# Layer 1's modulation scale on VectorE, for both condition vectors, in two column halves

## The chip, the cores and the metric

The kernel runs on one core of a Trainium2 chip. Each core has a matrix engine (TensorE, PE in the profile; PEld is its weight load), a vector engine (VectorE, DVE), an activation engine (ScalarE, ACT), a general engine (GpSimd, POOL) and a queue engine (SyncE, SP) that here issues the loads. Each engine works through its own instructions in a fixed order and waits where a semaphore tells it to. The metric is the device time of one execution, in microseconds (us), as the median of several runs. TensorE's full clock was granted for nearly all of the execution (0.984 of it on average).

## The reference

A stack of four layers on a sequence x and a context ctx, 256 tokens of 2048 channels each. Ahead of every layer, the two condition vectors c (for x) and c_ctx (for ctx) are turned into a shift, a scale and a gate of 2048 numbers each: one product of a vector with a 2048 x 6144 weight per layer.

```python
def ada_modulation(cond, w, b):
    m = jax.nn.silu(cond) @ w + b
    return jnp.split(m, 3, axis=-1)          # shift, scale, gate

for i in range(DEPTH):
    shift, scale, gate = ada_modulation(c, ada_w[i], ada_b[i])
    h = rms_norm(x, norm_g[i]) * (1.0 + scale[:, None, :]) + shift[:, None, :]
    shift_c, scale_c, gate_c = ada_modulation(c_ctx, ada_w[i], ada_b[i])
    hc = rms_norm(ctx, norm_g[i]) * (1.0 + scale_c) + shift_c
    # o, oc = mixer of h, hc: Fourier (layers 0, 3), window attention (1), gated convolution (2)
    x = x + gate[:, None, :] * o
    if i < DEPTH - 1:
        ctx = ctx + gate_c * oc
return rms_norm(x, final_g)
```

The modulation of layers 0 and 1 is needed for both condition vectors; in layer 1 the shift and the scale for both, the gate for c alone, because after layer 1 nothing reads the context any more. Layers 2 and 3 need c alone. Every weight is float32, and 429.56 MB are read from memory in one execution.

## The kernel before

Every large product (each layer's input products and its output product) streams its weight in pieces of [128, 2, 512] through SP's queue (`w_piece`, line 147). Each piece is split into a rounded part `whi` (ScalarE, line 183) and a rest `wlo` (VectorE, or GpSimd in some stages, line 184), and three matmuls (lines 196 to 198, or 216 to 218) multiply them with activations that are split the same way. A product takes 8 pieces for each of its 512-column chunks, and TensorE can start on a piece only when both parts of it are there.

The modulation runs in between. It is cut into **thirds** (l, s): layer l, and s = 0 for the shift, 1 for the scale, 2 for the gate. A third is 16 **row pieces**, each 128 rows of `ada_w` by 2048 columns, loaded as two tiles `aw` of 128 x 1024 (512 KB each, four buffers, line 331). Layer 0's shift and scale are made by `ada_tiles` (line 223). All other thirds belong to one of two streams:

- `ada_a` (line 373) works on TensorE: (0, 2), (1, 0), (1, 1). A row piece is four fp32 matmuls of 512 columns with the two condition vectors as the stationary operand (line 273), next to each other in the columns of the array, so both vectors are done at once. They show as eight records per row piece in the trace.
- `ada_v` (line 374) works on VectorE, for c alone: (1, 2), then all thirds of layers 2 and 3. A row piece is two operations over 128 x 1024: accumulator `adacc` plus `aw` times one number per partition (line 286; the first row piece only multiplies, line 284). During layer 2's gated product the stream is switched to TensorE (`ada_v.pe`, line 1084).

At the end of a third `ada_group` sums `adacc` over the partitions with four fp32 matmuls against a column of ones (line 300), where VectorE took part; copies the rows out of PSUM on ScalarE (line 303); turns them into columns with four small matmuls (line 305); and adds the bias (line 311) and, for a scale, the 1 and the norm's weight (line 315). `adacc` has one buffer: a third's first VectorE operation waits until the third ahead has been summed.

How far a stream is to be at which place is set by hand. A product calls a pump between its pieces, and `plan(quarters, steps)` spreads row pieces over those steps until so many quarters of a third (four row pieces each) are done. The constants (lines 27 to 36) are these goals, counted over the whole list of the stream: `TZ`, `T0U`, `T0O` for `ada_v` in layer 0's gate product z, its product u and its output product; `T1` up to layer 1's z product; `T1O` for its output product; `T2`, `T2Z`, `T2O` for layer 2's gated product, z product and output product. `A0Z` and `A0U` are the same for `ada_a`. `until(l, s)` emits whatever of a third is still missing, at the place where it is needed. In program order `until(1, 1)` stands ahead of the build of layer 1's input (line 808), `until(1, 2)` ahead of layer 1's output product (line 1040), `until(3, 1)` behind layer 2's output product (line 1173).

Program order is a priority, not the final order: a scheduler places every engine's instructions at compile time, and fills what it takes for free time of an engine with later work whose buffers are free. Weight splits and the builds at a layer's start get a higher priority (lines 178 and 466). So row pieces run well ahead of their place in the program, as far as the four `aw` tiles and the one `adacc` allow.

## Time and profile before

| | |
|---|---|
| median of 3 runs | 1947.56 us (1942.82 to 1949.57) |
| span of the profiled execution (first to last instruction) | 1946.4 us |
| TensorE matmuls, busy | 1866.9 us (96%) |
| VectorE, busy | 1425.8 us (73%) |
| ScalarE, busy | 891.3 us (46%) |
| GpSimd, busy | 280.8 us (14%) |
| loads by SP's queue | 429.99 MB, 67.2% of 16 DMA engines' time |
| modulation tiles `aw` loaded by the two streams | 320 of 512 KB |
| VectorE operations on `adacc` | 202 (188 of line 286, 14 of line 284) |
| records of line 273, of line 300, of line 305 | 472, 56, 80 |

The profile shows one execution. Busy time is the time in which an engine works on an instruction; matmuls are pipelined and overlap, so TensorE's busy time is no measure of its throughput. The chain of waits is found by going back from the last instruction, at each step to what released it. A row of a group of instructions has the line, the engine, the operation, what is written and read with its shape, the count, then the busy time, the mean time of one in ns, and the idle time of the engine just before them with its cause.

The stages, from where the accumulators of the products are first and last written: layer 0's z until 278 us, its u until 510, its output product until 726; layer 1's attention until about 963, its z until 1090, its output product until 1195; layer 2's gated product until 1397, its z with the layer norm until about 1510, its output product until 1615; layer 3 after that.

### The profile page before, as it was taken

To read this page: it belongs to the slowest core of one execution; us is meant where nothing else is said; L and a number is where in the kernel's file an instruction comes from. 1 tells how busy PE (TensorE), PEld (TensorE's weight loads), DVE (VectorE), ACT (ScalarE), POOL (GpSimd) and SP (SyncE) were. 2 spreads that over 40 slices of the span, in tenths; PEclk is the share of its full clock that TensorE was granted. 3 is DMA by queue.
4 is the path that set the end of the run, shared out by engine and by line. 5 is a ranking of instruction groups with operands and counts; after the bars stand their busy time and mean duration, and the time that the engine had idled before them with its cause. 6 is when DMAs were issued, how large, how long until landed. Compare 5 with 4: busy or idle time off the path is not lost.

```text
span 1946.4 us, 31356 instructions
## 1 busy us (share of the span) xinstructions
PE 1866.9 (96%) x11911; PEld 1552.1 (80%) x11911; DVE 1425.8 (73%) x2639; ACT 891.3 (46%) x1591; POOL 280.8 (14%) x143
## 2 busy tenths in 40 slices
PE   6999999999999999999999998999997997999997
PEld 5566657777766787766789997999997997888897
DVE  3799944556654459977897766688899968897665
ACT  6433342224322235465565444444445546556553
POOL 0000000000000000000000003889887001000000
PEclk9999999999999999999999999999998998999999
DMA  8888877676677845822567775577776785886564
GB/s 246 273 303 296 301 247 269 208 234 212 228 268 267 279 127 163 306 88 84 178 219 246 253 245 164 186 228 230 230 225 196 273 279 168 286 270 176 160 173 131
DMA packets 221129, 433.72 MB, mean 223 GB/s; under 512 B 14678, under 2 KB 85046, under 8 KB 220978
## 3 DMA queue, kind: packets, MB, share of 16 engines
q1 hardware_dynamic: 219552, 429.99, 67.2%
q8 instruction: 93, 1.52, 0.3%
q10 hardware_dynamic: 1426, 1.73, 0.3%
q14 instruction: 58, 0.48, 0.1%
HBM read 429.56 MB, written 2.10 MB: 222 GB/s over the span
## 4 chain that ended last, share of the span: by engine, by line
PE 81%; DVE 7%; DMA 6%; ACT 2%; issue 2%; SPq 1%; POOL 1%; DVEq 0%; ACTq 0%; POOLq 0%
PE acco L196 7%; PE acco L198 7%; PE acco L197 7%; PE accz L196 7%; PE accz L197 7%; PE accz L198 6%; PE accu L216 4%; PE accu L217 4%; PE accu L218 4%; DMA aw<-in_ada_w_dram 3%; PE pa L273 3%; PE accg L196 3%; PE accg L197 3%; PE accg L198 3%; PE po L968 2%
## 5 line engine op out<-in xcount | busy, mean ns | idle before, releaser
L183 ACT CAST whi<-raw 128x512 fp32r<-128x512 f32 (+1 forms) x748 | 538.4, 769 | 719.1 <-PE acco L197 200.4
L184 DVE TENSOR_TENSOR wlo<-raw,whi 128x512 fp32r<-128x512 f32 x648 | 472.5, 777 | 238.1 <-ACT whi L183 235.2
L184 POOL TENSOR_TENSOR wlo<-raw,whi 128x1024 fp32r<-128x1024 f32 x100 | 256.0, 2568 | 1348.7 <-ACT whi L183 1336.1
L196 PE MATMUL acco<-yh,whi 128*128 128x256 f32 (+1 forms) x1040 | 323.1, 311 | 0.0
L198 PE MATMUL acco<-yh,wlo 128*128 128x256 f32 (+1 forms) x1040 | 320.7, 309 | 0.8 <-DVE wlo L184 0.8
L286 DVE SCALAR_TENSOR_TENSOR adacc<-aw,csil,adacc 128x1024 f32<-128x1024 f32 x188 | 255.0, 1362 | 85.9 <-DMA aw<-in_ada_w_dram 85.5
L198 PE MATMUL accz<-hx,wlo 128*128 128x256 f32 x768 | 221.7, 289 | 14.1 <-POOL wlo L184 13.4
L197 PE MATMUL accz<-hx,whi 128*128 128x256 f32 x768 | 221.7, 289 | 3.8 <-DVE hx L448 3.8
L196 PE MATMUL accz<-hx,whi 128*128 128x256 f32 x768 | 221.3, 289 | 1.1 <-ACT hx L447 1.1
L196 PEld LDWEIGHTS acco<-yh,whi 128*128 128x128 f32 x1040 | 197.6, 190 | 27.1 <-ACT whi L183 11.2
L197 PE MATMUL acco<-yh,whi 128*128 128x256 f32 x768 | 217.5, 283 | 0.0
L1113 DVE SCALAR_TENSOR_TENSOR pv<-gp,dwT,pv 128x256 f32<-128x256 f32 x480 | 190.9, 484 | 24.9 <-ACT pv L1107 24.5
L198 PEld LDWEIGHTS acco<-yh,wlo 128*128 128x128 f32 x1040 | 197.5, 190 | 11.6 <-DVE wlo L184 1.9
L198 PEld LDWEIGHTS accz<-hx,wlo 128*128 128x128 f32 x768 | 150.9, 197 | 16.0 <-POOL wlo L184 13.8
L197 PEld LDWEIGHTS accz<-hx,whi 128*128 128x128 f32 x768 | 151.0, 197 | 5.7 <-DVE hx L448 4.4
L196 PEld LDWEIGHTS accz<-hx,whi 128*128 128x128 f32 x768 | 150.9, 197 | 3.8 <-ACT hx L447 1.8
L198 PE MATMUL accg<-hx,wlo 128*128 128x256 f32 x512 | 145.8, 285 | 1.9 <-POOL wlo L184 1.9
L196 PE MATMUL accg<-hx,whi 128*128 128x256 f32 x512 | 146.7, 287 | 0.6 <-ACT whi L183 0.4
L197 PEld LDWEIGHTS acco<-yh,whi 128*128 128x128 f32 x768 | 146.5, 191 | 0.0
L197 PE MATMUL accg<-hx,whi 128*128 128x256 f32 x512 | 145.8, 285 | 0.6 <-DVE hx L448 0.5
L196 PEld LDWEIGHTS accg<-hx,whi 128*128 128x128 f32 x512 | 98.9, 193 | 8.7 <-issue 6.9
L197 PE MATMUL acco<-yl,whi 128*128 128x512 f32 (+1 forms) x272 | 102.8, 378 | 0.0
(257 smaller groups left out, 3474.5 us busy)
## 6 DMA issues: line engine op xcount, KB each, us to landing
aw<-in_ada_w_dram SPq DMA_DIRECT2D x376, 512.0 KB, 5.3
raw<-in_four_w_in_dram SPq DMA_DIRECT2D x126, 512.0 KB, 4.6
raw<-in_attn_w_in_dram SPq DMA_DIRECT2D x72, 512.0 KB, 4.1
raw<-in_four_w_out_dram SPq DMA_DIRECT2D x64, 512.0 KB, 4.9
raw<-in_conv_w_in_dram SPq DMA_DIRECT2D x128, 256.0 KB, 3.0
raw<-in_attn_w_out_dram SPq DMA_DIRECT2D x32, 512.0 KB, 4.1
raw<-in_conv_w_in_dram SPq DMA_DIRECT2D x32, 512.0 KB, 4.1
raw<-in_conv_w_out_dram SPq DMA_DIRECT2D x32, 512.0 KB, 4.9
```

Of the source, the lines that this page charges most:

```text
L183: nc.scalar.copy(hv[:, c], iv[:, c])
L184: eng.tensor_sub(lv[:, c], iv[:, c], hv[:, c].bitcast(F32))
L196: mm(o, a, hh, start=st, stop=False, skip_group_check=True)
L197: mm(o, a, hl, start=False, stop=False, skip_group_check=True)
L198: mm(o, b, hh, start=False, stop=kt + k == span[1] - 1, skip_group_check=True)
L216: mm(acc[:], hh, whi[:, k, :], start=st, stop=False)
L217: mm(acc[:], hh, wlo[:, k, :], start=False, stop=False)
L218: mm(acc[:], hl, whi[:, k, :], start=False, stop=kt + k == KT - 1)
L273: mm(pa[32 * g:32 * g + cs.shape[-1], :], cs, aw[g // 2][:, 512 * (g % 2):512 * (g % 2) + 512], start=fp, stop=kt == KT - 1, skip_group_ch ...
L286: ins = nc.vector.scalar_tensor_tensor(acc[:, cs], aw[i][:], cc, acc[:, cs], op0=ALU.mult, op1=ALU.add)
L968: mm(po[64 * h:64 * h + 64, :256], vt[k][:, g * 64:(g + 1) * 64], pTs[h][:, k, :, :].rearrange("p m q -> p (m q)"), start=k == 0, stop=k == 3,
L1113: nc.vector.scalar_tensor_tensor(pv[:, :256], gt[:, t:t + 256], dwT[:, kt, t:t + 1], pv[:, :256], op0=ALU.mult, op1=ALU.add)
```

## The change

Third (1, 1) leaves `ada_a` and becomes the first of `ada_v`, under the name `BOTH`. It gets a function of its own, because VectorE has to make it for both condition vectors, which TensorE did at once: the 2048 numbers of the accumulator are now 1024 columns for c and the same 1024 columns for c_ctx, and the third is made in two column halves, one behind the other. A half is 16 tiles `aw` of 128 x 1024, and each tile feeds two VectorE operations, one per vector. Two tiles count as one row piece in the plans, so the third still has 16. Each half is summed, copied, turned and finished by itself. The goals of both streams change with it; since `ada_v`'s list is four quarters longer at its head, a goal of 24 now stands for what 20 was.

```diff
-A0U = 7.5
-T0U = 6.5
-T0O = 9
-T1 = 14.25
-T1O = 17.5
-T2 = 20.25
-T2Z = 21
-T2O = 21
+BOTH = (1, 1)
+A0U = 5.5
+T0U = 6
+T0O = 9.5
+T1 = 15
+T1O = 20
+T2 = 23.25
+T2Z = 24
+T2O = 24
...
-TZ = 3
+TZ = 2
...
+    def ada_both(l, s, st):
+
+        w = D // 2
+        for h in range(2):
+            acc = cp.tile([P, D], F32, tag="adacc", name=nm("adacc"))
+            for k2 in range(0, KT, 2):
+                for kt in (k2, k2 + 1):
+                    aw = st.half(l, s, kt, h)
+                    for o in range(2):
+                        cs, cc = slice(w * o, w * o + w), csil[:, kt, o:o + 1]
+                        if kt == 0:
+                            ins = nc.vector.tensor_scalar(acc[:, cs], aw[:], cc, None, op0=ALU.mult)
+                        else:
+                            ins = nc.vector.scalar_tensor_tensor(acc[:, cs], aw[:], cc, acc[:, cs],
+                                                                 op0=ALU.mult, op1=ALU.add)
+                if k2 < KT - 2:
+                    yield
+            pa = rs_bank("pa")
+            for g in range(4):
+                mm(pa[32 * g:32 * g + 32, :], one0[:], acc[:, 512 * g:512 * g + 512],
+                   start=True, stop=True, skip_group_check=True)
+            a = tmp()
+            nc.scalar.copy(a[:], pa[:])
+            for j in range(4):
+                mm(pa[:, 8 * j:8 * j + 8], a[:, j * P:(j + 1) * P], sel8[:], start=True, stop=True,
+                   skip_group_check=True)
+            c0 = 48 * l + 16 * s + 8 * h
+            for o in range(2):
+                dst = modc[l][:, 16 * s + 8 * h:16 * s + 8 * h + 8, o]
+                nc.vector.tensor_add(dst.rearrange("p (g j) -> p g j", g=2),
+                                     pa[:, :32].rearrange("p (j g o) -> p g j o", g=4, o=2)[:, 2 * o:2 * o + 2, :, 0],
+                                     adabT[:, c0:c0 + 8].rearrange("p (g j) -> p g j", g=2))
+                if s == 1:
+                    nc.vector.scalar_tensor_tensor(dst, dst, 1.0, ngT[:, 16 * l + 8 * h:16 * l + 8 * h + 8],
+                                                   op0=ALU.add, op1=ALU.mult)
+            yield
+        yield
...
+        def half(self, l, s, kt, h):
+            t = wp.tile([P, D // 2], F32, tag="aw", bufs=AWB, name=nm("aw"))
+            c0 = s * D + h * (D // 2)
+            nc.sync.dma_start(t[:], ada_w[l, kt * P:(kt + 1) * P, c0:c0 + D // 2])
+            return t
...
         def run(self):
             for l, s in self.todo:
-                yield from ada_group(l, s, self)
+                yield from (ada_both if (l, s) == BOTH else ada_group)(l, s, self)
...
-    ada_a = Stream(True, [(0, 2), (1, 0), (1, 1)])
-    ada_v = Stream(False, [(1, 2)] + [(l, s) for l in (2, 3) for s in range(3)])
+    ada_a = Stream(True, [(0, 2), (1, 0)])
+    ada_v = Stream(False, [BOTH, (1, 2)] + [(l, s) for l in (2, 3) for s in range(3)])
...
-    ada_a.plan(12, SA)
+    ada_a.plan(8, SA)
...
-                    ada_a.until(1, 1)
+                    ada_a.until(1, 0)
+                    ada_v.until(1, 1)
...
-    ada_v.plan(28, 60)
+    ada_v.plan(32, 60)
```

The rest of the diff removes comments.

## The prediction

> **What bounds the kernel now.** I read the page first, its span, its engine line and the shares of the chain, and took the prices of the two kinds of work from its groups of instructions.
>
> ```profile
> span 1946.4 us, 31356 instructions
> PE 1866.9 (96%) x11911; PEld 1552.1 (80%) x11911; DVE 1425.8 (73%) x2639; ACT 891.3 (46%) x1591; POOL 280.8 (14%) x143
> PE 81%; DVE 7%; DMA 6%; ACT 2%; issue 2%; SPq 1%; POOL 1%; DVEq 0%; ACTq 0%; POOLq 0%
> L273 PE MATMUL pa<-aw,csil 128*2 128x512 f32 x432 | 66.2, 598 | 0.9 <-DMA aw<-in_ada_w_dram 0.9
> L286 DVE SCALAR_TENSOR_TENSOR adacc<-aw,csil,adacc 128x1024 f32<-128x1024 f32 x188 | 255.0, 1362 | 85.9 <-DMA aw<-in_ada_w_dram 85.5
> ```
>
> TensorE is busy for 96% of the span and carries 81% of the chain; VectorE has about a quarter of the span free. L273 is the work that the change takes away from TensorE, L286 the kind that it adds to VectorE. An average over stages says little, so the second view is the busy time of the engines by stage (columns: stretch, its length, busy and count of PE, PEld, DVE, ACT, POOL, then clock, DMA share, GB/s).
>
> ```profile
> 54.00:278.00 224.00, 218.57 (x1041) 143.06 (x1042) 193.63 (x290) 89.09 (x113) 0.00 (x0) 0.99 0.84 285
> 278.00:510.00 232.00, 232.00 (x1197) 174.10 (x1200) 125.46 (x215) 71.03 (x132) 0.00 (x0) 1.00 0.71 237
> 510.00:726.00 216.00, 215.13 (x1083) 160.62 (x1076) 110.65 (x195) 60.72 (x120) 0.00 (x0) 1.00 0.69 233
> 963.00:1090.00 127.00, 127.00 (x1003) 115.54 (x1001) 99.03 (x188) 71.91 (x143) 0.00 (x0) 1.00 0.68 216
> 1090.00:1195.00 105.00, 102.06 (x812) 95.58 (x804) 71.02 (x112) 47.68 (x90) 8.52 (x7) 0.98 0.73 246
> 1195.00:1397.00 202.00, 197.78 (x1611) 188.21 (x1611) 163.50 (x393) 91.48 (x118) 165.80 (x86) 0.99 0.64 208
> 1460.00:1510.00 50.00, 35.44 (x267) 34.74 (x265) 49.30 (x73) 27.05 (x51) 37.73 (x11) 0.88 0.59 190
> 1510.00:1615.00 105.00, 98.43 (x802) 97.38 (x802) 85.65 (x132) 56.84 (x104) 9.49 (x4) 0.97 0.78 266
> ```
>
> The first three rows are layer 0: its gate product z, its product u, its output product. Then come layer 1's z and output products, layer 2's gated product, the end of its layer norm, and its output product. In layer 0's u and output products TensorE is busy for all but 0.9 us of 448, VectorE for 236. What is taken from TensorE there should shorten the path nearly one for one. Only at the end of layer 2's norm (1460 to 1510) does TensorE idle, 14.6 us, with VectorE full.
>
> **What is removed.** The third view is the chain of waits in order of time, inside layer 0's output product (start, length, what).
>
> ```profile
> 638.24 0.23 PE acco L198
> 638.46 0.97 PE pa L273 x8
> 639.43 0.43 PE acco L196
> 639.86 0.23 PE acco L197
> ...
> 645.10 0.97 PE pa L273 x8
> 646.07 0.86 PE pa L300 x8
> 646.93 0.43 PE acco L196
> 647.35 0.23 PE acco L197
> 647.58 0.24 PE acco L198
> 647.82 0.23 PE acco L196
> 648.05 0.79 PE pa L305 x8
> 648.84 0.33 PE acco L197
> ```
>
> A row piece of the modulation, four fp32 matmuls that the trace records as eight, takes 0.97 us of the chain, and the first product matmul behind it 0.43 in place of 0.23: 1.17 us a piece. Layer 1's scale third is 16 pieces: 18.7 us off TensorE. This is a cost on the path, not an average: nothing but product matmuls stands on either side.
>
> **What is added on TensorE.** The new third is summed over partitions twice, once a half: two more sets of L300, at most 1.17 each standing alone (0.86 behind a piece), 2.3 us together, and one more set of L305 than the old third had, 0.79 + 0.10 = 0.9 us. The plans also move: layer 2's gated product gets pieces up to 23.25 quarters from 20, thus 13, where it had 20.25 less 17.5, thus 11. Two more pieces, 2.3 us, in a stage where TensorE is busy for 197.78 of 202. The sum for TensorE is -18.7 + 2.3 + 0.9 + 2.3 = -13.2 us. The new reductions wait for VectorE's accumulation; behind one on TensorE stand the next product matmuls. L300 above starts with no gap after a piece, so I take that wait at nothing; ScalarE's extra copy of 128x512 and the short adds on VectorE are off the path.
>
> **What is added on VectorE.** The third is 64 operations, two condition vectors for each of 32 half pieces. Layer 2's two pieces more on TensorE are four operations fewer, so 60 in all. Priced by the middle duration of the view of the accumulator's instructions (count, ns min/median/max, first and last start):
>
> ```profile
> L286 DVE SCALAR_TENSOR_TENSOR adacc<-aw,csil,adacc x17: 1277/1280/1289, 1519.5 to 1575.0; 128x1024 f32<-128x1024 f32 x17
> ```
>
> 1.28 us each, 77 us, and VectorE goes from 1425.8 to about 1503 of the span: still not the bound as a whole. By stage, from the plans (an old piece is 2 operations, a piece of the new third 4): z of layer 0 goes from 3 quarters to 2 of the new kind, 24 to 32 operations, +8 or 10 us, against 30 us free. u goes from 28 to 48, +26 us against 107 free. The output product goes from 20 to 28, +10 against 105. Layer 1's output product goes from 3.25 quarters to 5, 26 to 40, +18 against 34. Layer 2's end must finish four pieces more before the boundary, because layer 3's scale has to be whole and the plan stops four quarters short of it instead of three: +8 operations, 10 us against 19 free in its output product. Everywhere the addition fits in the free time. I still charge 1 us each for z, layer 1's output product and layer 2's end, because a VectorE operation that waits for its load holds the weight rests (L184) behind it, and TensorE needs those. The bounds of each: 0 to the whole 10.2 us in z, where VectorE is at 86%; 0 to 2 in layer 1's output product and from 8.5 below nothing to 25 at layer 2's end, worked out with the rivals. In the three stages with most to spare TensorE ran full beside such operations already, so I stay near the lower ends. The new third itself is due at the end of layer 0's output product, where 9.5 quarters are planned and it needs 4; layer 1's gate, now behind it, is due before layer 1's output product, where 15 are planned and it needs 8. Neither can come late.
>
> **Transfers.** The third's 32 loads of 512 KB stay on SP's queue and in the same four buffers; only their place changes. Layer 0 loads 70 pieces of 1.05 MB instead of 84, an easing that I cost at nothing, since TensorE does not idle there. Layer 1's output product takes up to 7 pieces more: 246 GB/s for 105 us is 25.8 MB, with 7.3 more 33.1 MB, or 316 GB/s. The row of layer 0's z ran 285 GB/s at 0.84 share, so a full share would be 339: it fits, with little left.
>
> The sum is -13.2 + 3 = -10.2 us. The profiled execution's span is 1946.4 us, 1.2 below the median of the runs, 1947.56; I apply the difference to the median: 1937.4.
>
> **Rivals.** First, slower: layer 3's scale comes late. Its accumulator has one buffer, and the third ahead of it now ends on VectorE in layer 2's last z pieces; that third must be reduced on TensorE before the scale's first operation can start. How long such a turn can take shows around layer 1's z:
>
> ```profile
> L286 DVE SCALAR_TENSOR_TENSOR adacc<-aw,csil,adacc x7: 1275/1279/1280, 1022.2 to 1037.9; 128x1024 f32<-128x1024 f32 x7
> ```
>
> ```profile
> L300 PE MATMUL pa<-adacc,one x8: 592/604/617, 1089.5 to 1090.0; 128*32 128x512 f32 x8
> ```
>
> From the last operation to the reduction 52 us passed. In layer 2's output product 17 operations were spread from 1519.5 to 1575.0 (quoted above), 3.5 us from one to the next, since loads and weight rests stand between them. At that pace 32 need 111 us. They are wanted by 1608.1, where the trace has the reduction behind that product:
>
> ```profile
> 1608.10 1.06 PE L300 MATMUL pa<-adacc,one 128*32 128x512 f32 x8
> ```
>
> So they must start by 1497. The third ahead has six operations in the last z pieces, as the stage has now, and the sixth of those is at 1460.6 (quoted below). With a turn of 37 us nothing is late; one of 52 costs 15 and leaves the time 2 us above that of before; one of 60 costs 23, and the result is -13.2 + 23 = +10, 1957. It decides from 56 us on. Against it: from 1460 to 1510 TensorE idles, so the reduction can run at once. Chance 0.11.
>
> Second, slower too: the displaced operations fall where GpSimd works.
>
> ```profile
> 1457.04 3.28 DVE L286 SCALAR_TENSOR_TENSOR adacc<-aw,csil,adacc 128x1024 f32<-128x1024 f32 x1
> 1460.24 0.48 DVE L1113 SCALAR_TENSOR_TENSOR pv<-gp,dwT,pv 128x256 f32<-128x256 f32 x1
> 1460.63 3.04 DVE L286 SCALAR_TENSOR_TENSOR adacc<-aw,csil,adacc 128x1024 f32<-128x1024 f32 x1
> ```
>
> The same operation takes 3.28 and 3.04 us there, where GpSimd is busy for 37.73 of the 50 us from 1460. Eight more at 3.1 in a stretch where VectorE is the bound add 25 us, and the result is +12, 1959. The new third itself is safe: GpSimd's busy time in layer 0 is 0.00. The Trainium skill, SBUF — State Buffer, section "SBUF: two separate sides", says that VectorE and GpSimd share a pair of ports as an exclusive lock, so that one blocks wholly while the other runs an instruction; the two rows above agree with it. Against this rival, the plans put no more quarters into that stretch. Chance 0.06.
>
> Third, the saving is given back in small stalls. In z the added 10.2 us go half onto the path, 5. In layer 1's output product the turn of the accumulator bunches a whole third, 32 operations: VectorE 71.0 - 14 + 41 = 98 of 105 us, loads 36.3 MB, 107 us at 339 GB/s, 2 over. With 1 at layer 2's end that is 8, and the net is -5, 1942.4. Chance 0.20.
>
> Fourth, more than forecast: the turn pushes operations out of the chain of layer 2's norm.
>
> ```profile
> 1464.65 3.06 DVE adacc L286
> ...
> 1485.45 4.27 DVE adacc L286 x2
> ...
> 1492.18 1.18 DVE adacc L286
> ```
>
> These 8.5 us lie on the chain in the stretch where TensorE idles. If they move behind it, the result is -13.2 - 8.5 + 3 = -18.7, 1928.9. Chance 0.13. That the edit does not do what it says I leave out: the matmuls go with the list of thirds.
>
> **How the numbers follow.** The forecast itself, 1934 to 1941, has 0.50. Forecast and fourth rival are faster by more than 0.3% (5.8 us, about what a measurement of this kernel can tell from no change): 0.63. The third is within it: 0.20. The first two are slower: 0.17. The range reaches from the fourth rival to the first, 1928 to 1957, and leaves out the second and the tails.
>
> **What would show it.** Right: L273 falls from 59 pieces to 45, L300 grows from 7 sets to 9, VectorE's accumulator operations from 202 to 262; layer 0 ends 15 to 16 us earlier (18.7 less 3.2) with TensorE still full in u and the output product; layer 2's gated product is 2 us longer. Wrong: TensorE idles in layer 0's z behind L184 or L724; rows of TensorE waiting for L184 in layer 1's output product; the last operation of layer 3's scale starting after its output product ends; operations of 3 us on the norm's chain. The forecast fails if layer 0 is shorter but the later stages give the time back.

## The result, and the profile after

The kernel after takes 1959.0 us (median, 1954.48 to 1969.7), the kernel before 1947.56. The ratio is 1.006, with a 95% interval of 1.0044 to 1.0077: slower by 0.6%, some 12 us, where a gain of 10 was forecast. The profiled execution has a span of 1962.8 us; it took 1964.6 us and lies 5.6 above the median, so its stages show somewhat more loss than the median does. In the new file the lines named above are moved: 183 and 184 are 184 and 185, 196 to 198 are 197 to 199, 273 is 274, 286 is 287 (332 in the new function), 300 is 301 (338), 477 and 478 are 522 and 523. The runs below number the lines of their own files.

The page and its groups, by line:

```profile
span 1962.8 us, 31251 instructions
PE 1864.3 (95%) x11823; PEld 1559.1 (79%) x11823; DVE 1483.1 (76%) x2702; ACT 890.4 (45%) x1590; POOL 276.9 (14%) x143
PE 62%; DMA 11%; DVE 10%; issue 4%; ACT 1%; POOL 1%; SPq 0%; DVEq 0%; ACTq 0%; POOLq 0%
L274 PE MATMUL pa<-aw,csil 128*2 128x512 f32 (+1 forms) x360 | 50.6, 593 | 0.0
L287 DVE SCALAR_TENSOR_TENSOR adacc<-aw,csil,adacc 128x1024 f32<-128x1024 f32 x184 | 237.9, 1301 | 92.1 <-DMA aw<-in_ada_w_dram 91.2 <-DVE adacc L287 0.3
L332 DVE SCALAR_TENSOR_TENSOR adacc<-aw,csil,adacc 128x1024 f32<-128x1024 f32 x60 | 75.4, 1278 | 29.7 <-DMA aw<-in_ada_w_dram 29.7
```

The work moved as foreseen: 360 records are 45 row pieces, down from 59, and VectorE has its 60 operations more. But TensorE's part of the chain fell from 81% to 62%. Eleven of these points mean little: the chain of the kernel after is followed back to 216.6 us only, that of before nearly to the start. The other eight went to DMA, VectorE and "issue", which have ten points more together (ScalarE and SP have one less each): TensorE now waits. The mean of the old kind of VectorE operation even fell, from 1362 to 1301 ns: 2 of them take over 2 us in place of 8, so the slow operations beside GpSimd are fewer, not more. The busy time by stage, with the columns of the prediction's second view, says where:

```profile
278.00:508.50 230.50, 225.43 (x1132) 174.31 (x1128) 149.07 (x240) 70.63 (x131) 0.00 (x0) 0.99 0.64 213
508.50:720.00 211.50, 204.43 (x1001) 159.53 (x998) 117.31 (x196) 59.73 (x118) 0.00 (x0) 0.98 0.65 216
1086.00:1188.50 102.50, 99.38 (x800) 95.07 (x792) 87.80 (x126) 45.97 (x85) 3.41 (x2) 1.00 0.90 318
1518.00:1614.00 96.00, 95.44 (x785) 93.46 (x785) 83.21 (x124) 44.66 (x86) 0.00 (x0) 1.00 0.87 299
1614.00:1632.00 18.00, 7.67 (x32) 4.77 (x30) 9.53 (x17) 8.30 (x11) 7.86 (x3) 0.63 0.70 253
```

The first two rows are layer 0's u and output products. They had 0.9 us without TensorE in 448; now they have 12.1 in 442. The third is layer 1's output product, whose loads went from 246 to 318 GB/s; the last two are layer 2's output product and the boundary behind it. Taken from the starts of the products' first matmuls, in us:

| | layer 0 ends at | layer 1 to its output product | from there to layer 3's output product | span |
|---|---|---|---|---|
| before | 725.6 | 364.6 | 743.0 | 1946.4 |
| after | 720.4 | 366.0 | 763.6 | 1962.8 |

Layer 0 gave 5.2 us where 14.5 were forecast (15.5 less 1 in z), and the last group of stages took 20.6 where 4.3 were forecast. Within that group the gated product is 6.5 us longer, its z 7.5 shorter, layer 1's output product 6.4 longer and the boundary behind it 0.9, layer 2's output product and boundary 8.9, layer 3's first products 5.4. There are two questions, then: what holds TensorE in layer 0, and what lengthens the stages behind layer 1's attention?

### The profile page after: what moved, and what is told of

Read it like the earlier page. It is cut to its first block, busy times and chain, and to the rows that moved or that the text cites. A ratio compares the mean times of both kernels' runs of the same rounds, so it can differ in the third digit from the quotient of the medians.

```text
span 1962.8 us, 31251 instructions
## 1 busy us (share of the span) xinstructions
PE 1864.3 (95%) x11823; PEld 1559.1 (79%) x11823; DVE 1483.1 (76%) x2702; ACT 890.4 (45%) x1590; POOL 276.9 (14%) x143
## 4 chain that ended last, share of the span: by engine, by line
PE 62%; DMA 11%; DVE 10%; issue 4%; ACT 1%; POOL 1%; SPq 0%; DVEq 0%; ACTq 0%; POOLq 0%
DMA aw<-in_ada_w_dram 8%; PE acco L197 6%; PE acco L199 6%; PE acco L198 5%; PE accz L197 4%; PE accz L199 4%; PE accz L198 4%; DVE wlo L185 4%; PE accg L197 3%; PE accg L198 3%; PE accg L199 3%; PE accu L217 2%; PE accu L219 2%; PE accu L218 2%; PE po L1014 2%
## 5 line engine op out<-in xcount | busy, mean ns | idle before, releaser
L184 ACT CAST whi<-raw 128x512 fp32r<-128x512 f32 (+1 forms) x748 | 537.9, 770 | 703.2 <-PE acco L198 168.3
L287 DVE SCALAR_TENSOR_TENSOR adacc<-aw,csil,adacc 128x1024 f32<-128x1024 f32 x184 | 237.9, 1301 | 92.1 <-DMA aw<-in_ada_w_dram 91.2
L199 PEld LDWEIGHTS accz<-hx,wlo 128*128 128x128 f32 x768 | 151.6, 198 | 14.9 <-POOL wlo L185 11.5
L197 PEld LDWEIGHTS accg<-hx,whi 128*128 128x128 f32 x512 | 99.9, 195 | 12.1 <-issue 8.6
L217 PE MATMUL accu<-whi,hh 128*128 128x512 f32 x256 | 102.2, 399 | 4.2 <-DVE r L523 4.2
```

The source lines that it names most:

```text
L184: nc.scalar.copy(hv[:, c], iv[:, c])
L197: mm(o, a, hh, start=st, stop=False, skip_group_check=True)
L199: mm(o, b, hh, start=False, stop=kt + k == span[1] - 1, skip_group_check=True)
L217: mm(acc[:], hh, whi[:, k, :], start=st, stop=False)
L287: ins = nc.vector.scalar_tensor_tensor(acc[:, cs], aw[i][:], cc, acc[:, cs], op0=ALU.mult, op1=ALU.add)
```

## Experiments: what lengthens the later stages

Where the texts on record use letters for the theories, A is the turn of the accumulator, B the work added to VectorE, C the putting-off of pieces by the goals.

**The turn of the accumulator.** In layer 1's attention the trace shows a long turn of `adacc` (its tile view: line, count, ns min/median/max, first and last start):

```profile
L287 DVE SCALAR_TENSOR_TENSOR adacc<-aw,csil,adacc x17: 1273/1277/1286, 743.8 to 807.3; 128x1024 f32<-128x1024 f32 x17
L301 PE MATMUL pa<-adacc,one x2: 593/605/617, 839.7 to 840.1; 128*32 128x512 f32 x2
```

The last operation starts at 807.3; two of the eight records of its sum run at 840, and the other six only at 963, behind the attention. So 17 operations lie in this stretch where before had 33, and 32 move into layer 1's output product where before had 12. The first theory: the single accumulator's turn loses the time. In both kernels the summing matmuls were given a high priority.

```diff
-            for g in range(4):
-                mm(pa[32 * g:32 * g + 32, :], one0[:], acc[:, 512 * g:512 * g + 512],
...
+            with tc.high_priority(offset=1000):
+                for g in range(4):
+                    mm(pa[32 * g:32 * g + 32, :], one0[:], acc[:, 512 * g:512 * g + 512],
```

In the kernel after:

> The changed kernel, with the summing of a finished accumulator over the partitions (and its copy out) given a high priority, so that TensorE does it as soon as it can; nothing else differs. Theory A (the loss comes from the turns of the one accumulator: 161 us without an accumulator operation in layer 1's attention, 58 us at layer 2's end, and the bunching of loads and VectorE work behind each): the gap in the attention falls under 30 us, layer 1's output product goes back from 101.8 to about 96 us, layer 3's scale is whole before layer 2's output product ends, and the time is 1943 to 1950 us. Rival B (VectorE simply has too much to do, wherever it stands): under 3 us of change, 1956 to 1962.

In the kernel before:

> The kernel before, with the same priority for the summing. Theory A: the kernel before has turns of 50 to 90 us too, but its later stages did not wait for them, so 0 to 5 us faster, 1942 to 1948. If it gains as much as the changed kernel does by it (8 us or more), the turns are no cost of the change but of both.

After with it took 1979.0 us, a ratio to before of 1.0173 (1.0154 to 1.0192); before with it 1965.2, 1.0104 (1.0083 to 1.0124). The turn was short:

```profile
L303 PE MATMUL pa<-adacc,one x8: 592/604/617, 835.2 to 841.0; 128*32 128x512 f32 x8
L286 DVE TENSOR_SCALAR adacc<-aw,csil x2: 748/749/750, 854.0 to 856.5; 128x1024 f32<-128x1024 f32 x2
```

All eight records run by 841, the next third starts at 854, and layer 1's output product holds 7 operations in place of 32. The time is nevertheless 20 us longer, and so is that of before: the priority has a price of its own, which hides what a shorter turn is worth. Layer 1's output product with its boundary still took 110.5 us (104.9 before, 112.2 after), though its loads were at 0.70 of the DMA engines. The theory's forecast failed, by some 30 us, and that for the kernel before by 17; whether the turn costs anything by itself the two runs can't say.

**The goals.** A second theory looks at the constants. Since four quarters came in at the head of the list, the old goals would read 18.25, 21.5, 24.25, 25 and 25 from `T1` on; the change has 15, 20, 23.25, 24 and 24. So 3.25 quarters, 13 row pieces, that were due by layer 1's z are put off behind it, six of them behind layer 1's output product and four behind layer 2's too. Two runs: the kernel after without the putting-off (goals of layer 0 raised to 10.5 and 13 with them), and the kernel before, third still on TensorE, with the goals of after less four from `T0O` on (`TZ` 1 and `T0U` 4 lead up to them).

```diff
-T0U = 6
-T0O = 9.5
-T1 = 15
-T1O = 20
-T2 = 23.25
-T2Z = 24
-T2O = 24
+T0U = 10.5
+T0O = 13
+T1 = 18.25
+T1O = 21.5
+T2 = 24.25
+T2Z = 25
+T2O = 25
```

> The changed kernel with the goals of the VectorE stream put back to those of before, plus the four quarters of the new third (10.5, 13, 18.25, 21.5, 24.25, 25, 25): nothing of the later thirds is put off, and layer 0 takes all 64 added operations. Theory C (the loss comes from putting off later thirds, layer 1's output product and layer 2's end): layer 2's end and layer 1's output product are as before, and the time is 1935 to 1942. Theory A: about the same stages are mended if the turns fall well, 1940 to 1950. Rival B: layer 0 grows by 5 to 15 us from 28 more VectorE operations, 1960 or more.

```diff
-T0U = 6.5
-T0O = 9
-T1 = 14.25
-T1O = 17.5
-T2 = 20.25
-T2Z = 21
-T2O = 21
+T0U = 4
+T0O = 5.5
+T1 = 11
+T1O = 16
+T2 = 19.25
+T2Z = 20
+T2O = 20
...
-TZ = 3
+TZ = 1
```

> The kernel before (the scale third stays on TensorE), with the goals of the VectorE stream those of the change less the new third's four quarters (1, 4, 5.5, 11, 16, 19.25, 20, 20): the putting off alone, with no added VectorE work. Theories A and C: layer 1's output product and layer 2's end lose as in the changed kernel, together 10 to 15 us, with 7 us less in layer 2's z: 1950 to 1958. Rival B: no added VectorE work, so within 3 us of before, 1945 to 1950.

| | layer 0 ends at | layer 1 to its output product | from there to layer 3's output product | ratio to before |
|---|---|---|---|---|
| after, goals 10.5 to 25 | 734.3 | 366.2 | 746.9 | 1.0077 (1.005 to 1.0103) |
| before, put off | 719.8 | 366.8 | 760.3 | 1.009 (1.0068 to 1.0111) |

The late stages answer to the goals alone. Without the putting-off they take 746.9 us in the kernel after, close to the 743.0 of before; with it, and with no VectorE work added, the kernel before takes 760.3, and is 17.5 us slower as a whole. Its layer 1 output product is nearly that of the kernel after:

```profile
1087.00:1189.00 102.00, 98.93 (x791) 94.97 (x792) 87.26 (x126) 45.12 (x83) 3.37 (x2) 1.00 0.90 318
```

The loads take 0.90 of the DMA engines and 318 GB/s, and some of the product's own weights come late. In the kernel after (waits: engine, line, what it waited for, us in total, times, longest):

```profile
ACT whi L184 <- DMA raw<-in_attn_w_out_dram: 12.7, 7, 3.5
```

Before, the same wait came to 2.2 us. That is ScalarE's wait; how much of the 6.4 us it makes is not shown. TensorE itself waited 3.0 us there for `whi` and `wlo` (0.8 before), and one more sum and one more turn fell into the stage, 2.0 us.

The first of the two runs pays in layer 0 instead, where u is 12.3 us longer than before: 82 operations stand there, 48 in the kernel after. So theory C's time for it failed (1935 to 1942; it took 1960.5), though its late stages came as forecast, and what rival B had said of layer 0 happened: 8.7 us longer. Of the second run A and C had the direction right and 5 us too little, and B was wrong.

Three more sets of goals looked for the place where the 13 pieces fit: into u and layer 0's output product (7.5, 12, then 18.25 and on), the same with less in z (`TZ` 1, 6.5, 11.5, then 18.25 and on), and the last three goals alone (24.25, 25, 25).

```diff
-T0U = 6
-T0O = 9.5
+T0U = 7.5        # second run: 6.5, and TZ = 1
+T0O = 12         # second run: 11.5
-T1 = 15
-T1O = 20
+T1 = 18.25       # first and second run
+T1O = 21.5
-T2 = 23.25
-T2Z = 24
-T2O = 24
+T2 = 24.25       # all runs; the third has these three alone
+T2Z = 25
+T2O = 25
```

> The changed kernel with goals between: VectorE's stream at 2, 7.5, 12 quarters in layer 0, 18.25 at the end of layer 1's z, then as in e3_goals (21.5, 24.25, 25, 25). Layer 0's u loads as many pieces as before the change (36), not 48 as in e3_goals, and nothing later is put off. Theory C with an overloaded u as e3_goals' only loss: u at 226 to 231 us, output product at 208 to 212, the later stages as in e3_goals: 1938 to 1946. If any move of the goals costs, 1952 or more.

> As e7_goals_u7, with one quarter less in layer 0's z (1, 6.5, 11.5, then 18.25): 16 accumulator operations in z, where e4_defer with 8 was 6 us shorter than before with 24. Theory C: z 3 us shorter than in e7_goals_u7, u and output product the same within 2, layer 1's attention 0 to 2 longer: 1936 to 1944.

> The changed kernel with only the goals of layer 2 put back (24.25, 25, 25): TensorE makes the whole of layer 3's shift and one piece of its scale in the gated product, as before, and VectorE has 12 pieces left at the end instead of 16. Theory: the turn of the accumulator into layer 3's scale (58 us) goes, the scale is whole in time, and layer 2's output product, the boundary and layer 3's input products are back at 92, 13 and 212 us (13.9 us less); four pieces more on TensorE cost 4.7 us in the gated product; layer 2's z may grow back by up to 7.5. In all 1948 to 1956. If the late scale is not the cause, those three stages stay at 332 us together.

They took 1973.5 us (1.013, 1.0114 to 1.0147), 1953.1 (1.0039, 1.0023 to 1.0055) and 1959.8 (1.0062, 1.0045 to 1.0079). All three missed their forecasts. In the first TensorE idled 18.9 us in layer 0's output product, which took 229.5 us. In the second the late stages were as before (743.9 us), but layer 0's u and output products were 2.2 and 3.8 us longer than before, where they should have been shorter, and layer 1's attention 3.4. The third is telling: layer 2's end and layer 3 went back to the times of before, but layer 2's gated product and z together took 331.0 us where the kernel after has 319.5, and from layer 1's output product to layer 3's the sum is 763.2, that of the kernel after. In this run, once pieces had been put off past layer 1, raising the later goals only chose which stage pays.

So the goals were raised from `T1` on, with layer 0's left as the change has them (2, 6, 9.5):

```diff
-T1 = 15
-T1O = 20
-T2 = 23.25
-T2Z = 24
-T2O = 24
+T1 = 18.25
+T1O = 21.5
+T2 = 24.25
+T2Z = 25
+T2O = 25
```

> The changed kernel with its goals in layer 0 (2, 6, 9.5), then 18.25 at the end of layer 1's z and the rest as in e3_goals: layer 1's attention and z take 8.75 quarters instead of 5.5, so that nothing is put off beyond layer 1's z. Theory C: the stages from layer 1's output product on are as in e3_goals (within 4 us), layer 0 as in the changed kernel, and the attention and z pay for 13 more pieces, 2 to 12 us: 1944 to 1954.

1952.7 us, a ratio of 1.0023 (1.0012 to 1.0035), and 747.6 us from layer 1's output product to layer 3's, as in the first run without the putting-off. Layer 1's z pays back 5 of these 16 us, with 39 operations in place of 32. This much, 7 us by the ratios and 12 by the spans, is the price of the putting-off in the kernel after. Layer 0 still ended at 721.8.

## Experiments: where layer 0's saving went

**Is TensorE's term right?** In the kernel before the third (1, 1) was left out, with its loads, and its result set to 1 (`A0U`, the plan and the due place of `ada_a` follow as in the change).

```diff
...
-    ada_a = Stream(True, [(0, 2), (1, 0), (1, 1)])
+    ada_a = Stream(True, [(0, 2), (1, 0)])
+    nc.gpsimd.memset(modc[1][:, 16:32, :], 1.0)
...
```

> The kernel before with the scale third of layer 1 left out altogether: TensorE does not make it, VectorE neither (a constant stands for it, so the output is another one); the goals of the TensorE stream lose its four quarters, those of the VectorE stream stay. It measures the term of the sum by itself. If TensorE is what layer 0 lasts by, its u and output products shorten by 18.7 + 0.9 = 19.6 us together and the later stages stay: 1926 to 1932. If loads or VectorE hold layer 0 as well, less than 12 us show.

```profile
274.00:497.00 223.00, 222.89 (x1136) 173.08 (x1128) 127.69 (x218) 71.10 (x132) 0.00 (x0) 1.00 0.63 210
497.00:702.00 205.00, 202.03 (x1004) 158.33 (x1001) 107.38 (x188) 59.60 (x118) 0.00 (x0) 1.00 0.62 201
```

1925.3 us, 0.9889 (0.9874 to 0.9904). The u and output products are 8.9 and 10.3 us shorter, 19.2 in all, for the 18.7 + 0.9 that the prediction took for 16 pieces and a set of L305. The loads left out with it can hardly be the reason, since before TensorE waited for other engines and loads only 0.8 us in all in these two products. What is taken off TensorE here does shorten the path one for one, when nothing is put elsewhere.

**Is it VectorE's added work?** In the kernel after the second vector's multiplications were left out (all but the first of each half), with every load as it was.

```diff
                     for o in range(2):
+                        if o and kt:
+                            continue
                         cs, cc = slice(w * o, w * o + w), csil[:, kt, o:o + 1]
```

> The changed kernel with the second condition vector's multiplications left out beyond the first of each half, so that VectorE does 34 operations for the third instead of 64, with the same loads (the context's scale is wrong by that). If VectorE's added work eats layer 0's saving, layer 0 ends 6 to 10 us earlier than in the changed kernel, at 711 to 715 us. If it is loads that come late in VectorE's order, layer 0 changes by less than 4 us. Later stages lose by the putting off as in the changed kernel, within 5 us.

1952.6 us, 1.0027 (1.0014 to 1.0039): 30 operations of 1.28 us less, 38 us of VectorE, gave 6 us. Layer 0 ended at 708.6 in its profiled execution, which was however 9.6 us below this kernel's median, so only the ratio is used. VectorE's part in layer 0 it confirms; whether the amount or the order of its work counts it leaves open. All that was left out fell into z and u: in u TensorE has no such wait any more, while in the output product, which kept its 31 operations, it still waits 5.3 us at one place.

**The order on VectorE.** The trace has the place. VectorE's row in the order of time, in layer 0's u product of the kernel after (start, length, what, and in brackets the idle time before it and its cause), and TensorE's at the same moment:

```profile
325.18 1.29 DVE L185 TENSOR_TENSOR wlo<-raw,whi 128x512 fp32r<-128x512 f32 x2
326.38 0.68 DVE L523 TENSOR_TENSOR r<-accu,r 128x512 fp32r<-128x512 f32 x1
332.92 1.28 DVE L332 SCALAR_TENSOR_TENSOR adacc<-aw,csil,adacc 128x1024 f32<-128x1024 f32 x1 [5.85 <-DMA aw<-in_ada_w_dram]
334.12 0.68 DVE L523 TENSOR_TENSOR r<-accu,r 128x512 fp32r<-128x512 f32 x1
```

```profile
330.30 0.39 PE L219 MATMUL accu<-whi,hl 128*128 128x512 f32 x1
334.86 0.61 PE L217 MATMUL accu<-whi,hh 128*128 128x512 f32 x1 [4.17 <-DVE r L523]
```

VectorE has nothing to do for 5.85 us. A multiplication stands at the head of its queue and waits for its load; the short operation `r` (0.68 us), the last that has to read the finished accumulator before TensorE can start the next one in it, stands behind it, and TensorE waits 4.17 us. The Trainium skill, Perfetto Trace Analysis, section "Tensor Engine Instruction (MATMUL, LD_WEIGHTS)", says that the queues of ScalarE, VectorE and GpSimd are strictly first in, first out, and only TensorE's can pull weight loads ahead; these rows agree, 5.85 us of it.

The second such place is at 520 us:

```profile
520.13 1.28 DVE L287 SCALAR_TENSOR_TENSOR adacc<-aw,csil,adacc 128x1024 f32<-128x1024 f32 x1 [6.08 <-DMA aw<-in_ada_w_dram]
521.34 1.28 DVE L185 TENSOR_TENSOR wlo<-raw,whi 128x512 fp32r<-128x512 f32 x2
522.70 1.28 DVE L287 SCALAR_TENSOR_TENSOR adacc<-aw,csil,adacc 128x1024 f32<-128x1024 f32 x1
523.90 1.97 DVE L567 TENSOR_TENSOR tmp<-pb,tmp 128x512 f32<-128x512 f32 x2
```

```profile
525.66 0.58 PE L577 MATMUL pm<-r,dfth 128*128 128x258 f32 x1 [4.88 <-ACT r L522]
```

VectorE idles 6.08 us in front of a multiplication; behind it stand two weight rests, one more multiplication and `tmp`, on which ScalarE and then the matmuls `pm` of the Fourier step depend, and TensorE waits 4.88. These two waits are 9.0 of the 12.1 us. The kernel before has waits of VectorE for `aw` too, 70.0 us of them in these two products (87.4 after). But TensorE lost at most 1.0 us to all of them. Of the 15 over 2.5 us, 12 have a weight rest next behind them, which is made ahead of its use; of the other three one has an `r` (3.59 us at 510). That the next operation is a weight rest is no safety by itself, as the place at 520 shows: what counts there is `tmp` a little farther back.

If the order counts, then the same operations, in the same stages, need only stand elsewhere. In u and the output product each multiplication was tied behind the latest weight rest of the program, and each piece loaded one step ahead:

```diff
-                eng.tensor_sub(lv[:, c], iv[:, c], hv[:, c].bitcast(F32))
+                rest = eng.tensor_sub(lv[:, c], iv[:, c], hv[:, c].bitcast(F32))
+                if eng is nc.vector:
+                    pin[1] = rest
...
+    def paced(ins):
+        if pin[0]:
+            tc.add_manual_dep(ins.ins, pin[1].ins.name,
...
+    pin[0] = True
...
+    pin[0] = False
...
+            ahead = [st.half(l, s, kt, h) for kt in (0, 1)]
             for k2 in range(0, KT, 2):
+                now, ahead = ahead, [st.half(l, s, kt, h) for kt in (k2 + 2, k2 + 3) if kt < KT]
                 for kt in (k2, k2 + 1):
-                    aw = st.half(l, s, kt, h)
+                    aw = now[kt - k2]
...
+                        paced(ins)
```

(`paced` and the early load stand in `ada_group` in the same way; the dependence only fixes the order on the one engine, it is no wait.)

> The changed kernel with its goals, but in layer 0's u and output products each piece of the VectorE stream is loaded one pump step before its multiplications, and these may not stand ahead of the latest weight rest in VectorE's order. If late loads at the head of VectorE's queue eat layer 0's saving (the two stalls of 4 and 5 us), layer 0 ends 6 to 10 us earlier than in the changed kernel, at 711 to 714. If the four buffers are the limit, loads of the other stream come later in turn, and layer 0 ends at 718 or later.

1946.1 us, 0.9996 (0.9984 to 1.0008): 12.5 us faster than after by the ratios, and layer 0 ends at 702.7, beyond what was expected. The order was then tried without the early loads (the lines with `ahead` taken out again), and both together in the kernel before as a control (the same edit there, in `ada_group` alone):

> The kernel after with only one half of the mending of layer 0: the multiplications stand behind the latest weight rest, but each piece is loaded when its own step comes, not a step ahead. If the order on VectorE is what cost layer 0 its saving, this alone brings it: layer 0 ends at 700 to 708 and the time is 1943 to 1950. If it is the late load, whatever the order, VectorE still waits at the head of its queue and the stalls at 330 and 520 us remain: layer 0 ends at 714 to 722, the time is 1954 to 1962.

> A control: the kernel before, its third still on TensorE, with the same order in layer 0's u and output products (multiplications behind the latest weight rest, loads one step ahead). If the order only takes away stalls that the change brought, there is little to take in before, whose u and output products have 1.0 us of stalls together: 1943 to 1950, layer 0 ending at 720 to 727. If the order is a gain of its own whatever stands on VectorE, layer 0 ends 10 us or more earlier and the time is 1932 to 1940.

```profile
325.79 0.69 DVE L535 TENSOR_TENSOR r<-accu,r 128x512 fp32r<-128x512 f32 x1 [0.67 <-ACT r L534]
327.15 0.69 DVE L535 TENSOR_TENSOR r<-accu,r 128x512 fp32r<-128x512 f32 x1 [0.67 <-ACT r L534]
329.91 1.30 DVE L193 TENSOR_TENSOR wlo<-raw,whi 128x512 fp32r<-128x512 f32 x2 [2.06 <-ACT whi L192]
331.12 4.87 DVE L343 SCALAR_TENSOR_TENSOR adacc<-aw,csil,adacc 128x1024 f32<-128x1024 f32 x4
```

```profile
279.00:502.50 223.50, 223.39 (x1136) 173.28 (x1128) 149.84 (x241) 70.67 (x131) 0.00 (x0) 1.00 0.67 219
502.50:705.00 202.50, 201.80 (x1009) 158.56 (x1002) 116.98 (x197) 59.85 (x118) 0.00 (x0) 1.00 0.67 226
```

This is the run with the order alone: VectorE around the first place, where both `r` now run ahead of the multiplications, and the u and output products by stage. VectorE is busy for 149.84 and 116.98 us, as in the kernel after (149.07 and 117.31), and TensorE is full again. The time is 1948.0 us, 1.0012 (0.9997 to 1.0027): the order does it, and the early load adds nothing that these intervals tell apart. The order does two things at once: the operations that TensorE needs soon stand ahead, and VectorE waits less for `aw` (31.2 us in the two products in place of 87.4), since a multiplication that stands later more often finds its load landed. How much each of the two gives is not shown. In the kernel before order and early loads are no gain but a small loss, 1953.5 us, 1.0033 (1.0017 to 1.005), with layer 0 ending at 727.3 and the two products 6.8 us longer, 5.4 of them in the row pieces on TensorE: it is a cure for what the change brought, not a gain of its own. Which half of the edit costs this in the kernel before was not tried. The time of u and the output product, as the sums of the times from each TensorE matmul's start to the next, in us:

| what TensorE works on | before | after | order alone |
|---|---|---|---|
| row pieces of the modulation | 43.3 | 26.1 | 25.1 |
| sums and turns of a third | 5.9 | 6.3 | 6.3 |
| the two products' own matmuls | 359.8 | 371.3 | 357.0 |
| the Fourier matmuls (`pm`, `pb`) | 36.6 | 37.5 | 36.1 |

The pieces gave 17.2 us, as the change meant it. The 0.4 of the sums is no measure of the new third's, since one of its two halves was summed and turned in layer 0's z, at 250 us. The kernel after gave 12.4 of that back in the other two rows, which hold the same matmuls in all three kernels.

## Experiments: both mended

**Both at once.** If there are two separate causes, their removals add. The first try had the goals raised from `T1` on (18.25, 21.5, 24.25, 25, 25) and the order with early loads, and `pin[0] = False` stood only ahead of layer 1's output product:

> The kernel after with both mendings at once: in layer 0's u and output products each multiplication stands behind the latest weight rest and its piece is loaded one step ahead, as in the run before this one that did it alone (1946.07, layer 0 ending at 703), and from layer 1 on the goals are raised so that nothing is put off (18.25, 21.5, 24.25, 25, 25, as in the run with the later goals alone, where layer 1's output product to layer 3's norm took 747.6 us against 762.2). If the loss has these two separate causes, their removals add: 1946.1 less 14.6 is 1931.5, so 1927 to 1936, faster than before by 0.6 to 1%, and layer 0 still ends at 700 to 708. If the two are one loss that only moves (what layer 0 gains must be made up later), the run stays at 1942 to 1950.

1949.5 us, 1.0019 (1.0005 to 1.0032), not 1931.5. Layer 0 ended at 705.1 and the late stages took 749.4 us, both as foreseen, but layer 1's z took 146.3 us in place of 127 to 133. Its queue waits (SP) and ScalarE's:

```profile
SPq L387 <- DVE adacc L298: 53.6, 33, 5.1
```

```profile
ACT whi L192 <- DMA raw<-in_attn_w_in_dram: 27.5, 9, 5.6
```

A multiplication that stands later frees its `aw` buffer later. SP waits for that buffer, and behind it on SP's queue stand the weights of the product itself. With the order kept to layer 0, and in the second run the goals of layer 0 changed too:

```diff
+    pin[0] = False       # behind layer 0, in both
...
-TZ = 2               # second run alone
-T0U = 6
-T0O = 9.5
+TZ = 1
+T0U = 6.5
+T0O = 11.5
```

> Both mendings again (goals 18.25, 21.5, 24.25, 25, 25 from layer 1 on; the order on VectorE and the load one step ahead), but the order is kept to layer 0. In the run with both, where the order held until layer 1's output product, layer 0 ended at 705 and layer 1's output product to layer 3's norm took 748.6 us, as forecast, but layer 1's z took 146.3 us against 127 to 133: multiplications that stand later free their buffers later, SP waits 53.6 us to issue the next piece (9.1 in before) and the product's own weights stand behind it on SP's queue (ScalarE waits 27.5 us for them). If that is the whole of the difference, layer 1's z takes 127 to 135 us here, layer 0 still ends at 702 to 708, and 705 + 74 + 162 + 132 + 748 + 113 is a span of 1934, a time of 1931 to 1940. If the pieces that are not put off cost as much wherever they go, another stage is longer by 10 us or more and the time is 1943 to 1951.

> The same as the run beside it with layer 0's goals at 1, 6.5 and 11.5 in place of 2, 6 and 9.5: eight pieces fall into layer 0's output product instead of layer 1's z. If loads fit there as long as VectorE's order is kept, layer 0 ends at 706 to 716 with no TensorE stall over 1 us, layer 1's z takes 126 to 130, and the time is within 4 us of the run beside it, 1931 to 1941. If SP's queue is what these loads fill, as in layer 1's z, layer 0's output product takes 215 us or more and the time is 1943 or more.

The first took 1937.6 us (1935.1 to 1941.6), a ratio of 0.9959 (0.9945 to 0.9974): faster than before and than after, and within a microsecond of the time that the prediction had given for the change. Layer 0 ends at 701.9, layer 1's z takes 133.2, and from layer 1's output product to layer 3's it is 751.9 us. The same two waits in that z:

```profile
SPq L387 <- DVE adacc L298: 35.6, 24, 3.8
```

```profile
ACT whi L192 <- DMA raw<-in_attn_w_in_dram: 5.8, 3, 2.9
```

The two mendings alone were worth 12.5 and 7.2 us by their ratios; together 1.006 less 0.9959 is 1.0%, 19.7 us. They add, as well as these intervals (2 to 3 us either way for each ratio) can tell. The second of the two took 1947.1 us, 1.0002 (0.9988 to 1.0016), as its rival had it, but not by the rival's stage (215 us or more for the output product): eight pieces more in layer 0 lengthened u from 222.5 to 235.4 and the output product from 203.5 to 208.7. Of these 18 us, two row pieces that moved there from z on TensorE and one more sum with its turn are about 8; the rest is spread over the products' own matmuls in stalls below 2 us each, which I did not take apart.

## Why the prediction was wrong

- **TensorE's term** was right. 18.7 us for the pieces: 17.2 in the kernel after and 18.2 with the order alone on the pieces' own records, 19.2 with all that hangs on the third, where it was left out altogether. A piece is 1.1 us, for 1.17. What the sums of the new third cost, charged with 3.2 us, the runs don't give by itself.
- **"Everywhere the addition fits in the free time"** is the step that failed. VectorE did keep 81 us free in u and 94 in the output product, and TensorE still lost 12.1 there. The prediction itself named the mechanism, an operation that waits for its load and holds what stands behind it, but charged 1 us for it in z, layer 1's output product and layer 2's end, and nothing in u and the output product "with most to spare". It also looked at the wrong follower: TensorE waited for `r` and `tmp`, which are made just when they are needed, and not for the weight rests of L184. That TensorE ran full beside such operations before was true of 51 operations there; with 79 some came to stand ahead of these two. The order alone took away 11.3 of the 12.1 us, with VectorE as busy as it was.
- **The goals** were read as numbers of pieces per stage and costed by busy time and by GB/s. Layer 1's output product, charged with 0 to 2, took 6.4. The check of its loads came out right (316 GB/s forecast, 318 measured) and the conclusion, that it fits below 339, did not: at 0.90 of the DMA engines ScalarE waited 12.7 us for the product's weights, and TensorE 2.2 us more than before for `whi` and `wlo`. The 339 was no ceiling either: from 1129 to 1178 us, inside that product, a slice of the page moves 348. Layer 2's gated product, charged with 2.3 us for two pieces more, took 6.5: 12 pieces ran in it in place of 7.75 (3.9 us), because in before 2.25 had run ahead of it in layer 1's output product (1 after) and one behind it, and its own matmuls took 3.6 more. In all the putting-off cost 7 to 12 us here, and 17.5 in the kernel before by itself.
- **The third rival** had that stage's mechanism, a whole third of 32 operations bunched in it; 32 were counted. Its price of 2 us was a third of the truth.
- **The first rival** happened at its threshold. Layer 3's scale waited from 1463.0, the last operation ahead of it, to a sum at 1521.3, a turn of 58 us where it was to decide from 56. It was to be shown by an operation of that scale that starts after the product's end, and one does. At the end of the product TensorE waits:

```profile
1463.03 3.04 DVE L287 SCALAR_TENSOR_TENSOR adacc<-aw,csil,adacc 128x1024 f32<-128x1024 f32 x1
...
1521.28 1.06 PE L301 MATMUL pa<-adacc,one 128*32 128x512 f32 x8
...
1613.51 3.75 DVE L287 SCALAR_TENSOR_TENSOR adacc<-aw,csil,adacc 128x1024 f32<-128x1024 f32 x3 [0.28 <-DVE adacc L287]
1618.35 0.42 DVE L462 TENSOR_TENSOR ss<-ss,tmp 128x256 f32<-128x256 f32 x1
...
1621.40 1.02 PE L472 MATMUL pss<-ones,ss 128*128 128x1 f32 x4 [6.77 <-DVE ss L462]
```

  Its price was 8.9 us, not the 21 of its sum: 5.0 in the boundary and 3.9 in layer 2's output product ahead of it. The wait of 6.77 is not all new; in before TensorE waited 5.0 us at that place, for ScalarE's copy of the scale's sum. **The fourth rival** happened beside it: operations left the chain of the norm, and z became 7.5 us shorter (8.5 forecast). I had taken the two for alternatives; they are two ends of the same shift, and nearly cancel. **The second** did not happen: only 2 of these operations take over 2 us in the whole execution, where before had 8. That its time, 1959, is the measured one is chance.
- The forecast's time came true in another kernel, 1937.6 for 1937.4, but that is partly chance: there layer 0 gave 23.7 us instead of 14.5, and all behind it took 14 instead of 4.3.

What is left open: whether the long turn of the accumulator costs anything apart from the pieces that it displaces, since the priority that shortened it has its own price; and why layer 3's first products took 5.4 us more with the pieces put off (3 to 6 us in the runs that kept all the change's goals), which was not traced to an instruction.

## What to carry to other kernels

Free time of an engine is no cover for work on it that waits for a load: ask what stands behind that operation in its engine's order, and how far ahead of its use each follower is made. A follower that is made just in time can turn most of the wait into a stall (4.2 of 5.9 us and 4.9 of 6.1 here). Putting the same work behind it brought all of that back in layer 0, but it is not free everywhere: it cost 13 us in layer 1's z. When work is added at the head of a list with due times, every later due time has moved too: cost that shift apart, by running it alone in the old kernel, before costing the work.

## What the runs showed that I had not expected

Layer 1's output product with its boundary took 107.2 to 113.9 us in the ten kernels whose loads took 0.88 to 0.90 of the DMA engines there, and 104.3 to 106.8 in the seven with 0.64 to 0.73, so it suffered before the engines were full. It is no strict rule: the kernel after with the priority had 0.70 and took 110.5. And a buffer that is freed a little later reaches far: SP's wait for `aw` of 53.6 us in place of 35.6 in layer 1's z, by an order that had been free in layer 0 of the kernel after, cost that stage 13 us.
